# Four shared tiles with a float32 and a float32r name for what is transposed, in a two-layer hybrid decoder trunk

## Chip, core and metric

The kernel runs on one core of a Trainium2 chip. The metric is the device time of one execution in microseconds. An execution of the kernel before takes 2374.29 us (median of 3 runs, 2373.88 to 2375.04).

The core has five engines with a queue each, which the profile names PE (TensorE: matrix products and transposes; PEld is its load of the stationary operand), DVE (VectorE), ACT (ScalarE), POOL (GpSimd) and SP (SyncE, here an issuer of transfers). SBUF is the working memory, PSUM the memory that TensorE writes.

## The reference

Two layers over x of 256 positions by 2048 channels, float32, each followed by a SwiGLU FFN of hidden width 5632.

```python
for layer in range(2):
    h = rms_norm(x, mix_norm[layer])
    if layer == 0:
        z, xbc, dt_raw, c_q, c_kv, k_rope = split(h @ w_in)
        y_ssd = ssd_mixer(z, xbc, dt_raw, ...)   # conv(xbc), silu, chunked scan, rms_norm(y * silu(z))
        y_mla = mla_mixer(c_q, c_kv, k_rope, ...) # rms_norm(c_q) @ w_uq, rms_norm(c_kv) @ w_ukv, rope, softmax
        mix = concat(y_ssd, y_mla) @ w_out_even
    else:
        mix = stick_breaking_mixer(h, w_qkv, w_out_odd)   # 16 heads of 128, weights from a reversed cumsum
    x = x + mix
    h = rms_norm(x, ffn_norm[layer])
    x = x + (silu(h @ w_gate) * (h @ w_up)) @ w_down
return rms_norm(x, final_norm)
```

## The kernel before

**Precision.** A float32 product of full accuracy is made from float32r operands (the type that TensorE streams faster): each operand is split into a high part, cast to float32r by ScalarE (L330), and a low part, the rest, by VectorE (L336). Three products hi x hi, hi x lo and lo x hi are summed in PSUM. Weights arrive from HBM in tiles of 128 x 4 x 512 words (1 MB), and every tile is split so. Small products, in attention heads and the scan, are made in plain float32.

**Products.** `project` (L433) makes two 128 x 512 blocks with 16 steps of six matmuls (L440, L442, L443), one step for each 128 rows of the weights. `pair` (L733) makes two neighbouring blocks of 512 columns at once by a scheme of seven products in place of eight, M1 to M7, on part of the depth, with plain products (c0 to c3) for the rest; its matmuls have line L770. The sums of M1, M5, M6 and M7 are copied out of their bank in between ("kept", L791) and are handed later to the callbacks `left` and `right`, which add the bank's final sum to them. HALF, MORE and LATE are three orders of the same work.

**Order.** TensorE's instructions run in the order in which the program writes them. The order on the other engines is a planner's, from priorities and estimated times; `urgent` gives an instruction a high priority, and weight casts of later tiles are issued after urgent instructions. Work that has to happen while a product runs (transposes, heads, scan steps) is written as a generator; `tick` is called once or twice a step of a product and advances those that are due, and `yield n` means n ticks later. So a transpose that "waits 10" is put into TensorE's stream ten ticks into the product that follows.

**Tiles.** Most temporaries come from one pool of 42 tiles of 128 x 512 words (`s2`, named `s` in the profile). A tile is given back when all that read it are done. One arena holds the weight slots and the residual; the residual's four blocks have two names for the same memory, `xres` (float32) and `xwords` (float32r).

**Transposes.** A transpose is a TensorE instruction with the tile as the stationary operand and an identity as the moving one; its result goes to a PSUM tile `tr`. Four of 128 x 128 fill a block. `transpose` (L338) takes the float32r path (L341, `ident_r`) if the source has that type and the float32 path (L343, `ident`) if not. On the float32 path before:
- L379, `transpose_plain`: q and k of the stick-breaking layer, two tasks one after the other
- L343 on `s`: the latents c_q and c_kv and the four gated outputs of the scan
- L1338, `conv`: the inputs of the convolution, six blocks
- L1478, `evac_rope`: the rotated queries of MLA, four groups
- L343 on `xres`, L1407, L1513, L1371 and some single ones.

On the float32r path: the residual (`xwords`), and the gated tiles of the FFN (`ident_r,s`). For the latter, `right` multiplies into the tile of silu(gate) (L915), then a transfer from GpSimd's queue copies that tile into a float32r tile (L918), which is transposed ten ticks into the next product.

Of the kernel before, what the change touches and what calls it, by code (L numbers as in the profile page):

```python
# [15 lines left out]
P = 128  # L16
# [22 lines left out]


class Trunk:

# [81 lines left out]
    def weight_slots(self):  # L124
# [4 lines left out]
        base = -(-nc.sbuf_base // 256) * 256  # L129
        nc.alloc_sbuf_tensor("arena", [P, n * 2048 + 4096], F32, align_bytes=256)  # L130
        self.slots = {"wh": [], "w": [], "wsum": []}
# [11 lines left out]
        self.xres = [x(j, "xres", F32) for j in range(4)]  # L143
        self.xwords = [x(j, "xwords", F32R) for j in range(4)]

        self.saved = [self.dp.tile([P, 2, 512], F32, name=f"saved{j}") for j in range(4)]
# [225 lines left out]
    def transpose_plain(self, src, res, wait=4):  # L372

        for k2 in range(2):
            yield wait if k2 == 0 else 1
            pt = self.tr([2, S])
            for k in range(2):
                for t in range(2):
                    self.nc.tensor.transpose(pt[:, k, t * P:(t + 1) * P], src(t, 2 * k2 + k), self.ident)  # L379
# [352 lines left out]

    def pair(self, st, va, vb, left, right, order=HALF, after=lambda m: None):  # L733

# [39 lines left out]
        def add(b, x, w, keep=None):  # L774
# [13 lines left out]
            if keep:  # L788
                with self.urgent():
                    o = kept[keep] = self.s2([512])  # L790
                    copied = nc.scalar.copy(o, ps[b]).ins  # L791
# [107 lines left out]
    def ffn(self, layer, st, gain_next):  # L899
# [13 lines left out]
        def right(t, c, s):  # L913
            nc.vector.tensor_tensor(s, c, s, op=ALU.add)
            nc.vector.scalar_tensor_tensor(h[t], s, rstd[:, t:t + 1], h[t], op0=ALU.mult, op1=ALU.mult)  # L915

            words = self.s2([512], F32R)
            nc.gpsimd.dma_start(words.bitcast(F32), h[t])  # L918
            h[t] = words

        def gate_up(n):
            self.pair(st, self.cols(wg, n * 512), self.cols(wu, n * 512), left, right,
                      self.MORE if n >= 3 else self.HALF,
                      lambda m: st["lo"] if n == 0 and m in ("M3", "M6") else None)
# [75 lines left out]
    def stick(self, st):  # L1000
# [4 lines left out]
        for g in range(4):  # L1005
            raw = [[None, None], [None, None]]
            self.pair(st, cols(0, g), cols(1, g), take(raw[0]), take(raw[1]))
            qk, wts = [], []
            for r in raw:
# [70 lines left out]
    def scaled(self, st, func=AF.Copy):  # L1080

        nc = self.nc

        def to(res):
            def take(t, c, s):
                if "rstd" not in st:
                    st["rstd"] = self.norm_end(st)
                nc.vector.tensor_tensor(s, c, s, op=ALU.add)
                nc.scalar.activation(s, s, func, scale=st["rstd"][:, t:t + 1])
                res[t] = s  # L1090
            return take
# [52 lines left out]
    def even(self, st):  # L1144
# [6 lines left out]
        for n in (4, 5, 0, 1, 2, 3):  # L1151
            ps = self.project(xT, self.cols(win, OFF_XBC + n * 512, first=n == 4), KD)
            if n == 4:
                self.late_vectors()
                rstd = self.norm_end(st)
            raw = self.evac(ps, AF.Copy, rstd)
            res = []
            conv[n] = (self.spawn(self.conv(raw, n, res)), res)
            if n == 4:
# [6 lines left out]
        for off, g in ((OFF_CQ, self.g_q), (OFF_CKV, self.g_kv)):  # L1166
            ps = self.project(xT, self.cols(win, off), KD)
            raw = self.evac(ps, AF.Copy, rstd)
            ssq = self.small([P, 2], "ssqc")
# [6 lines left out]
            cT.append((self.spawn(self.transpose_split(  # L1176
                lambda t, k, raw=raw: raw[t][:, k * P:(k + 1) * P], res, g, 6)), res))
        ssq_u = self.small([P, 2, 4], "ssq")
        uT = self.operand()
        for n in range(4):  # L1180
# [3 lines left out]
            for t in range(2):  # L1184
                nc.gpsimd.tensor_tensor(y[n][t], y[n][t], sz[t], op=ALU.mult)
                if n < 3:
                    self.square_sum(y[n][t], ssq_u[:, t, n:n + 1])
            src, g = lambda t, k, n=n: y[n][t][:, k * P:(k + 1) * P], self.g_ssd[:, 4 * n:4 * n + 4]
            if n < 2:
# [7 lines left out]
        def root():  # L1197
            yield 7
            for t in range(2):
                with self.tc.issue_after(self.kept):  # L1200
                    self.square_sum(y[3][t], ssq_u[:, t, 3:4])
            yield 4
# [20 lines left out]
    def dt_and_krope(self, rstd, xT):  # L1223
# [74 lines left out]

        self.kpeT = self.small([P, 2, S], "kpeT", bufs=1)
        nc.vector.memset(self.kpeT, 0.0)  # L1300
# [12 lines left out]
    def apply_rope(self, dst, src, t, h):  # L1313
# [4 lines left out]
        a, b = src[:, :, 0:32], src[:, :, 32:64]  # L1318
        t1, t2 = (self.small([P, h, 32], f"rope{c}{h}") for c in "ab")
# [4 lines left out]
        t1, t2 = (self.small([P, h, 32], f"rope{c}{h}") for c in "ab")  # L1324
# [4 lines left out]
    def conv(self, raw, n, res):  # L1329

        nc = self.nc
        for k2 in range(2):
            yield (8 if n == 4 else 2) if k2 == 0 else 1
            pt = self.tr([2, S])
            for k in range(2):
                for t in range(2):
                    c = (2 * k2 + k) * P
                    nc.tensor.transpose(pt[:, k, t * P:(t + 1) * P], raw[t][:, c:c + P], self.ident)  # L1338
            o = self.s2([2, S])
# [92 lines left out]
    def mla_group(self, g, cq, ckv, oT):  # L1432
# [11 lines left out]

        qp = self.evac_rope(self.project(cq, heads(wuq, 128, 64), 4, 256))
        q = self.project_T(cq, heads(wuq, 0, 128))
# [16 lines left out]

    def evac_rope(self, ps):

        nc = self.nc
        rp, res = self.s2([2, 4, 64]), []
        qp = self.s2([2, 4, 64])
# [4 lines left out]
        def gen():  # L1473
            yield 7
            pt = self.tr([2, S])
            for h in range(2):
                for t in range(2):
                    nc.tensor.transpose(pt[:, h, t * P:(t + 1) * P],  # L1478
                                        rp[:, t, 2 * h:2 * h + 2].rearrange("p a d -> p (a d)"), self.ident)
            o = self.s2([2, S])  # L1480
# [93 lines left out]
```

## Time and profile before

| | |
|---|---|
| time, median of 3 | 2374.29 us |
| time of the profiled execution | 2374.24 us |
| its span, first to last instruction | 2372.2 us |
| DMA | 497.88 MB, mean 210 GB/s |
| largest group on VectorE | L336 on w, x399, 895.9 us |
| largest group on ScalarE | L330 from w, x399, 744.2 us |
| instructions of GpSimd | 301 |

Busy time of an engine is the union of its instructions; matmuls are pipelined, so the next begins before the last ends, and a busy TensorE need not be at its peak. A group of the profile is given by line, engine, operation, output and inputs by the program's names, shape, count, then busy time, mean duration in ns, and the idle time of the engine just ahead of it with what ended that idle time.

### The profile page before, as it was taken

The numbers are of one execution on the slowest core, as the hardware profiler recorded it, in microseconds if no ns is written. First come the engines' busy times: TensorE is split into PE (matmuls) and PEld (weight loads), VectorE is DVE, ScalarE is ACT, GpSimd is POOL, SyncE is SP. The second block draws the span as 40 slices with busy tenths as digits, with TensorE's granted clock in tenths as the row PEclk, the third lists the DMA queues.
The fourth block names the chain that finished last, engine by engine and source line by source line (L and its number), as shares of the span: only waits on it lengthen the run. The fifth ranks groups of instructions, "written<-read, shape, count | busy, mean of one in ns | idle before, by whom it ended". The sixth has DMA issues, their size and how long they took to land.

```text
span 2372.2 us, 28286 instructions
## 1 busy us (share of the span) xinstructions
PE 2354.9 (99%) x11083; PEld 1959.4 (83%) x11083; DVE 1987.8 (84%) x1639; ACT 1458.9 (62%) x1476; POOL 227.2 (10%) x301
## 2 busy tenths in 40 slices
PE   9999999999999999999999999999999999999998
PEld 7888888988888888888888888888888888888886
DVE  6786587588998889989888889779997988999884
ACT  6665565566665665566665686776665666556663
POOL 1341011110000000000000000000000000000011
PEclk9999999999999999999999999999999999999999
DMA  7665556445667777777776555556667777777773
GB/s 270 205 199 178 179 195 190 131 142 195 231 223 213 236 225 229 225 236 225 230 240 220 200 167 177 179 174 234 229 229 220 224 236 229 226 223 238 224 258 114
DMA packets 274917, 497.88 MB, mean 210 GB/s; under 512 B 22940, under 2 KB 48160, under 8 KB 274784
## 3 DMA queue, kind: packets, MB, share of 16 engines
q1 hardware_dynamic: 255264, 446.20, 57.2%
q0 software_dynamic: 18752, 48.55, 7.7%
q8 instruction: 87, 1.43, 0.2%
q10 hardware_dynamic: 768, 1.33, 0.2%
q14 instruction: 46, 0.38, 0.0%
HBM read 459.24 MB, written 25.20 MB: 204 GB/s over the span
## 4 chain that ended last, share of the span: by engine, by line
PE 89%; issue 6%; DVE 2%; ACT 2%; POOL 0%; DMA 0%; SPq 0%; POOLq 0%; ACTq 0%; DVEq 0%
PE acc L770 51%; PE acc L440 11%; PE acc L443 11%; PE acc L442 10%; PE acc L484 1%; DVE w L336 1%; ACT wh L330 1%; PE tr L341 1%; PE at L1423 1%; PE acc L486 0%; DVE wsum L717 0%; PE tr L343 0%; DVE wsum L336 0%; PE at L1495 0%; PE at L1496 0%
## 5 line engine op out<-in xcount | busy, mean ns | idle before, releaser
L336 DVE TENSOR_TENSOR w<-w,wh 128x2048 fp32r<-128x2048 f32 (+2 forms) x399 | 895.9, 2253 | 191.4 <-ACT wh L330 186.2
L770 PE MATMUL acc<-wh,s 128*128 128x512 f32 x3896 | 985.6, 391 | 4.2 <-ACT s L791 2.6
L330 ACT CAST wh<-w 128x2048 fp32r<-128x2048 f32 (+2 forms) x399 | 744.2, 1874 | 331.0 <-PE acc L443 154.1
L770 PEld LDWEIGHTS acc<-wh,s 128*128 128x128 f32 x3896 | 725.4, 188 | 154.2 <-ACT s L791 4.3
L440 PE MATMUL acc<-wh,s 128*128 128x512 f32 (+1 forms) x1216 | 483.6, 398 | 0.0
L443 PE MATMUL acc<-wh,s 128*128 128x512 f32 (+1 forms) x1216 | 471.5, 388 | 0.0
L442 PE MATMUL acc<-w,s 128*128 128x512 f32 (+1 forms) x1152 | 445.9, 387 | 0.0
L770 PE MATMUL acc<-w,s 128*128 128x512 f32 x1312 | 355.8, 390 | 0.5 <-DVE w L336 0.4
L770 PEld LDWEIGHTS acc<-w,s 128*128 128x128 f32 x1312 | 246.0, 188 | 53.1 <-DVE w L336 1.7
L443 PEld LDWEIGHTS acc<-wh,s 128*128 128x128 f32 x1216 | 228.7, 188 | 47.7
L440 PEld LDWEIGHTS acc<-wh,s 128*128 128x128 f32 x1216 | 228.9, 188 | 44.9 <-issue 1.7
L442 PEld LDWEIGHTS acc<-w,s 128*128 128x128 f32 x1152 | 217.1, 188 | 42.3 <-issue 1.7
L336 DVE TENSOR_TENSOR wsum<-wsum,wh 128x2048 fp32r<-128x2048 f32 (+1 forms) x101 | 218.1, 2160 | 6.3 <-ACT wh L330 6.3
L330 ACT CAST wh<-wsum 128x2048 fp32r<-128x2048 f32 (+1 forms) x101 | 182.7, 1809 | 50.2 <-PE acc L770 26.6
L330 ACT CAST wh<-lent 128x2048 fp32r<-128x2048 f32 (+1 forms) x62 | 114.5, 1857 | 61.7 <-PE acc L443 24.0
L336 DVE TENSOR_TENSOR lent<-lent,wh 128x2048 fp32r<-128x2048 f32 (+1 forms) x62 | 137.1, 2217 | 10.4 <-ACT wh L330 10.2
L717 DVE TENSOR_TENSOR wsum<-w,wsum 128x2048 f32<-128x2048 f32 (+1 forms) x52 | 104.3, 2005 | 20.2 <-PE acc L770 18.2
L791 ACT COPY s<-acc 128x512 f32<-128x512 f32 x132 | 77.3, 587 | 70.6 <-PE acc L770 70.6
L770 PE MATMUL acc<-wsum,s 128*128 128x512 f32 x380 | 104.6, 390 | 0.3 <-DVE wsum L336 0.3
L918 POOL DMA_DIRECT2D s<-s x44 | 24.4, 556 | 808.9 <-DVE s L915 465.4
L935 POOL DMA_DIRECT2D saved<-s x64 | 56.5, 1010 | 314.7 <-ACT s L934 313.6
L770 PEld LDWEIGHTS acc<-wsum,s 128*128 128x128 f32 x380 | 71.2, 188 | 16.0 <-DVE wsum L336 1.1
(270 smaller groups left out, 1924.7 us busy)
## 6 DMA issues: line engine op xcount, KB each, us to landing
w<-in_w_down_dram SPq DMA_DIRECT2D x80, 1024.0 KB, 4.9
w<-in_w_gate_dram SPq DMA_DIRECT2D x76, 1024.0 KB, 5.1
w<-in_w_up_dram SPq DMA_DIRECT2D x76, 1024.0 KB, 5.2
w<-in_w_qkv_dram SPq DMA_DIRECT2D x48, 1024.0 KB, 5.0
w<-in_w_in_dram SPq DMA_DIRECT2D x47, 1024.0 KB, 5.2
w<-in_w_out_even_dram SPq DMA_DIRECT2D x32, 1024.0 KB, 4.9
saved<-s POOLq DMA_DIRECT2D x64, 256.0 KB, 7.3
w<-in_w_out_odd_dram SPq DMA_DIRECT2D x16, 1024.0 KB, 4.9
```

The source lines that it names most:

```text
L330: cast = nc.scalar.copy(hi, src).ins
L336: return nc.vector.tensor_tensor(lo, src, hi.bitcast(F32), op=ALU.subtract).ins
L341: self.nc.tensor.transpose(out.bitcast(F32R), src, self.ident_r)
L440: nc.tensor.matmul(ps[t], hi[:, ts], wh, start=k == 0, stop=False)
L442: slot.used(nc.tensor.matmul(ps[t], hi[:, ts], wl, start=False, stop=False), self.clock)
L443: nc.tensor.matmul(ps[t], lo[:, ts], wh, start=False, stop=k == nk - 1)
L484: nc.tensor.matmul(ps[:, h % 2], wh[:, hs], x, start=k == n == 0, stop=False)
L717: ins = self.nc.vector.tensor_tensor(half(o, so), half(p, sp), half(q, sq), op=ALU.subtract).ins
L770: m = nc.tensor.matmul(ps[b], x, y, start=b not in started, stop=stop, skip_group_check=True)
L791: copied = nc.scalar.copy(o, ps[b]).ins
L918: nc.gpsimd.dma_start(words.bitcast(F32), h[t])
L935: nc.gpsimd.dma_start(self.saved[n][:, t], s, accum_op=ALU.add)
```

## The change

Four tiles (`twins`) of 128 x 512 words are laid out in the arena, each with two names for the same memory, `raw` (float32) and `words` (float32r). Engines write `raw`; TensorE transposes `words`. They are not from the pool: there is one buffer of each, so a new write waits for the readers of the last. Twins 2 and 3 share their memory with `kpeT` and with the scratch of the rotation, which are used in the first mixer only and leave the pool `small`. The pool `acts` has 40 tiles in place of 42.

- FFN: the kept sums M1 and M7 go to twins 2 and 3, where silu is applied in place; `right` multiplies into twins 0 and 1. The copy by transfer (L918) is gone.
- Stick-breaking layer: q goes to twins 0 and 1, k to twins 2 and 3.
- First mixer: convolution inputs, latents and gated outputs go to twins 0 and 1, the rotated queries to twin 0 or 1 in turn.

```diff
+class Twin:
+    def __init__(self, raw, words):
+        self.raw, self.words = raw, words
...
-        self.ap = ec(tc.tile_pool(name="acts", bufs=42))
+        self.ap = ec(tc.tile_pool(name="acts", bufs=40))
...
+        self.kpeT = more("kpeT", [P, 2, S], 2)
+        self.rope4 = {c: [more(f"rope{c}4{q}", [P, 4, 32], 3, 1024 * m + 512 * q) for q in range(2)]
+                      for m, c in enumerate("ab")}
+        self.twins = [Twin(more(f"twin{t}", [P, 512], t), more(f"twinwords{t}", [P, 512], t, 0, F32R))
+                      for t in range(4)]
...
 (transpose_plain)
-                    self.nc.tensor.transpose(pt[:, k, t * P:(t + 1) * P], src(t, 2 * k2 + k), self.ident)
+                    self.transpose(pt[:, k, t * P:(t + 1) * P], src(t, 2 * k2 + k))
...
-    def evac(self, ps, func=AF.Copy, scale=None):
+    def evac(self, ps, func=AF.Copy, scale=None, twins=None):
...
-            o = self.s2([512])
+            o = twins[t].raw if twins else self.s2([512])
...
 (pair)
-                    o = kept[keep] = self.s2([512])
+                    o = kept[keep] = homes[keep] if keep in homes else self.s2([512])
...
 (ffn)
-            nc.vector.scalar_tensor_tensor(h[t], s, rstd[:, t:t + 1], h[t], op0=ALU.mult, op1=ALU.mult)
-
-            words = self.s2([512], F32R)
-            nc.gpsimd.dma_start(words.bitcast(F32), h[t])
-            h[t] = words
+            nc.vector.scalar_tensor_tensor(self.twins[t].raw, s, rstd[:, t:t + 1], h[t], op0=ALU.mult, op1=ALU.mult)
...
+                      {"M1": self.twins[2].raw, "M7": self.twins[3].raw})
...
-                lambda t, k, h=tuple(h): h[t][:, k * P:(k + 1) * P], res, wait=10 if n < HID // 512 - 1 else 6, rank=self.URGENT)), res
+                lambda t, k: self.twins[t].words[:, k * P:(k + 1) * P], res, wait=10 if n < HID // 512 - 1 else 6, rank=self.URGENT)), res
...
 (stick, and scaled, which writes twins[t].raw where it is given twins)
-            self.pair(st, cols(0, g), cols(1, g), take(raw[0]), take(raw[1]))
+            self.pair(st, cols(0, g), cols(1, g), take(twins=self.twins[:2]), take(twins=self.twins[2:]))
...
-                    lambda t, k, r=r: r[t][:, k * P:(k + 1) * P], res)), res))
+                    lambda t, k, r=r: r[t].words[:, k * P:(k + 1) * P], res)), res))
...
 (even)
-            raw = self.evac(ps, AF.Copy, rstd)
+            raw = self.evac(ps, AF.Copy, rstd, self.twins)
...
-                nc.gpsimd.tensor_tensor(y[n][t], y[n][t], sz[t], op=ALU.mult)
+                nc.gpsimd.tensor_tensor(self.twins[t].raw, y[n][t], sz[t], op=ALU.mult)
...
 (conv)
-                    nc.tensor.transpose(pt[:, k, t * P:(t + 1) * P], raw[t][:, c:c + P], self.ident)
+                    self.transpose(pt[:, k, t * P:(t + 1) * P], self.twins[t].words[:, c:c + P])
...
 (evac_rope)
-                    nc.tensor.transpose(pt[:, h, t * P:(t + 1) * P],
-                                        rp[:, t, 2 * h:2 * h + 2].rearrange("p a d -> p (a d)"), self.ident)
+                    self.transpose(pt[:, h, t * P:(t + 1) * P], twin.words[:, (2 * t + h) * P:(2 * t + h + 1) * P])
```

More of the change, by code (lines that the diff above doesn't have):

```diff
@@ L144, in weight_slots @@
         self.xwords = [x(j, "xwords", F32R) for j in range(4)]
+        more = lambda name, shape, t, o=0, dt=F32: nc.alloc_sbuf_tensor_at(
+            name, shape, dt, offset=base + 8192 * n + 16384 + 2048 * t + o).ap()
+        self.kpeT = more("kpeT", [P, 2, S], 2)
[3 more added lines that the diff above has]
+                      for t in range(4)]
         self.saved = [self.dp.tile([P, 2, 512], F32, name=f"saved{j}") for j in range(4)]
@@ L731, with pair @@
     LATE = ("M1", "M5", "M3", "M6", "M2", "M7", "M4", "c0", "c1", "c2", "c3")
-    def pair(self, st, va, vb, left, right, order=HALF, after=lambda m: None):
+    def pair(self, st, va, vb, left, right, order=HALF, after=lambda m: None, homes={}):
         nc = self.nc
@@ L1082, in scaled, with to @@
         nc = self.nc
-        def to(res):
+        def to(res=None, twins=None):
             def take(t, c, s):
@@ L1088, in take @@
                 nc.vector.tensor_tensor(s, c, s, op=ALU.add)
-                nc.scalar.activation(s, s, func, scale=st["rstd"][:, t:t + 1])
-                res[t] = s
+                o = twins[t].raw if twins else s
+                nc.scalar.activation(o, s, func, scale=st["rstd"][:, t:t + 1])
+                if res:
+                    res[t] = s
             return take
@@ L1167, in even @@
             ps = self.project(xT, self.cols(win, off), KD)
-            raw = self.evac(ps, AF.Copy, rstd)
+            raw = self.evac(ps, AF.Copy, rstd, self.twins)
             ssq = self.small([P, 2], "ssqc")
@@ L1176, in even @@
             cT.append((self.spawn(self.transpose_split(
-                lambda t, k, raw=raw: raw[t][:, k * P:(k + 1) * P], res, g, 6)), res))
+                lambda t, k: self.twins[t].words[:, k * P:(k + 1) * P], res, g, 6)), res))
         ssq_u = self.small([P, 2, 4], "ssq")
@@ L1200, in root @@
                 with self.tc.issue_after(self.kept):
[L1201 removed]
+                    self.square_sum(self.twins[t].raw, ssq_u[:, t, 3:4])
             yield 4
@@ L1318, in apply_rope, with pair @@
         a, b = src[:, :, 0:32], src[:, :, 32:64]
-        t1, t2 = (self.small([P, h, 32], f"rope{c}{h}") for c in "ab")
+        def pair():
+            if h != 4:
+                return tuple(self.small([P, h, 32], f"rope{c}{h}") for c in "ab")
+            for c in "ab":
+                self.rope4[c].append(self.rope4[c].pop(0))
+            return tuple(self.rope4[c][1] for c in "ab")
+        t1, t2 = pair()
         tt = nc.gpsimd.tensor_tensor
@@ L1323, in apply_rope @@
         tt(dst[:, :, 0:32], t1, t2, op=ALU.subtract)
-        t1, t2 = (self.small([P, h, 32], f"rope{c}{h}") for c in "ab")
+        t1, t2 = pair()
         tt(t1, a, sin, op=ALU.mult)
```

22 lines of the change are left out of this document (10 added, 12 removed).

## Prediction, made before the result was known

> **What bounds the kernel now.** I read the page first, then TensorE's waits, then the busy time by stage.
>
> ```profile
> span 2372.2 us, 28286 instructions
> PE 2354.9 (99%) x11083; PEld 1959.4 (83%) x11083; DVE 1987.8 (84%) x1639; ACT 1458.9 (62%) x1476; POOL 227.2 (10%) x301
> PEclk9999999999999999999999999999999999999999
> ```
> ```profile
> engine line waited for: us in total, times, longest us
> PE acc L770 <- ACT s L791: 2.6, 3, 1.2
> PE tr L293 <- DVE s L253: 1.8, 1, 1.8
> PE acc L770 <- ACT wh L330: 1.6, 1, 1.6
> PE tr L341 <- PE tr L341: 0.9, 1, 0.9
> PE tr L343 <- DMA xres<-in_x_dram: 0.6, 1, 0.6
> PE acc L770 <- DVE w L336: 0.4, 2, 0.2
> PE acc L770 <- DVE wsum L336: 0.3, 1, 0.3
> ```
> ```profile
> 34.00:205.00 171.00, 171.00 (x866) 142.12 (x867) 129.83 (x232) 107.36 (x121) 54.11 (x59) 1.00 0.60 199
> 410.00:520.00 110.00, 109.57 (x759) 100.93 (x757) 66.59 (x110) 63.78 (x132) 23.48 (x43) 1.00 0.49 148
> 640.00:1190.00 550.00, 550.00 (x2474) 455.22 (x2473) 493.91 (x305) 327.92 (x255) 37.65 (x50) 1.00 0.73 226
> 1340.00:1580.00 240.00, 237.99 (x1126) 198.93 (x1125) 199.55 (x160) 174.22 (x213) 18.00 (x16) 1.00 0.53 173
> ```
>
> The columns of the last block are: stretch and its length, then busy time with count of TensorE, weight load, VectorE, ScalarE and GpSimd. TensorE is busy 99% of the span at the full granted clock. All that it waited for another instruction or a transfer adds up to 2.6 + 1.8 + 1.6 + 0.9 + 0.6 + 0.4 + 0.3 = 8.2 us, and 2.4 of these (the idle tile of L253 and the first load of x) belong to the start. In the convolution stretch it is busy 171.00 of 171.00 us, in the first FFN 550.00 of 550.00. So the rule for this change is simple: an edit counts if it makes TensorE's own queue shorter, or if it puts a wait into that queue. What the other engines gain is not seen in the end time.
>
> **What gets shorter: 176 transposes.** The diff gives four tiles a second, float32r name, so five groups of transposes leave the float32 path (ident) for the float32r path (ident_r). The rows of these groups, and the one of the FFN's activations that take the float32r path already:
>
> ```profile
> L341 PE MATMUL tr<-ident_r,s 128*128 128x128 f32 x176 | 20.1, 237 | 0.0
> L379 PE MATMUL tr<-ident,s 128*128 128x128 f32 x64 | 8.3, 272 | 0.0
> L343 PE MATMUL tr<-ident,s 128*128 128x128 f32 x48 | 7.4, 273 | 0.0
> L1338 PE MATMUL tr<-ident,s 128*128 128x128 f32 x48 | 7.2, 272 | 0.0
> L1478 PE MATMUL tr<-ident,s 128*128 128x128 f32 x16 | 2.4, 272 | 0.0
> ```
>
> These are q and k (L379), the latent and gated outputs (L343), the convolution inputs (L1338) and the rotated queries (L1478): 64 + 48 + 48 + 16 = 176. Other float32 transposes (L1407, L1513 and a few more) are left as they are. The mean duration of one, 272 against 237 ns, is not the price: transposes overlap, and what counts is by how much a group pushes back the matmuls behind it. This is read from the timeline, in two places where a group of four, then four 128x512 matmuls of L770, then the next group of four follow each other. First float32, then float32r (columns: start, duration of the merged row, instructions):
>
> ```profile
> 612.76 0.60 PE L343 MATMUL tr<-ident,xres 128*128 128x128 f32 x4
> 613.11 1.17 PE L770 MATMUL acc<-wh,s 128*128 128x512 f32 x4
> 614.12 0.60 PE L343 MATMUL tr<-ident,xres 128*128 128x128 f32 x4
> ```
> ```profile
> 707.51 0.85 PE L770 MATMUL acc<-w,s 128*128 128x512 f32 x3
> 708.20 0.46 PE L341 MATMUL tr<-ident_r,s 128*128 128x128 f32 x4
> 708.49 1.16 PE L770 MATMUL acc<-wh,s 128*128 128x512 f32 x4
> 709.49 0.46 PE L341 MATMUL tr<-ident_r,s 128*128 128x128 f32 x4
> ```
> ```profile
> 1347.52 1.03 PE L379 MATMUL tr<-ident,s 128*128 128x128 f32 x8
> 1348.31 1.17 PE L770 MATMUL acc<-wh,s 128*128 128x512 f32 x4
> 1349.32 0.93 PE L379 MATMUL tr<-ident,s 128*128 128x128 f32 x7
> ```
>
> From group to group the float32 case takes 614.12 - 612.76 = 1.36 us, the float32r case 709.49 - 708.20 = 1.29 us, with the same four matmuls inside. Four transposes become 0.07 us cheaper (0.06 to 0.08 within the rounding of the starts). A matmul of L770 takes (708.20 - 707.51) / 3 = 0.23 us, so four transposes cost 1.36 - 0.92 = 0.44 us in float32 and 0.37 in float32r.
>
> In the stick-breaking layer the transposes of q and k stand together, eight at a time (the third block; its last row is cut at seven by the end of the window): 1349.32 - 1347.52 - 0.92 = 0.88 us for eight. In float32r eight should cost at most twice four, 0.74, and at least 8 x (708.49 - 708.20) / 4 = 0.58, plus the 0.37 - 0.29 = 0.08 us by which the matmul behind a group is late, 0.66. They save 0.14 to 0.22; I take 0.17, nearer to the price of the fours, which is measured.
>
> The sum: 112 transposes outside the stick-breaking layer are 28 groups of four, 28 x 0.07 = 2.0 us; 64 in it are 8 groups of eight, 8 x 0.17 = 1.4 us. Together 3.4 us, all on TensorE's queue, which does not wait where they stand (171.00 of 171.00; 109.57 of 110.00; 237.99 of 240.00). From the bounds: 28 x 0.06 + 8 x 0.14 = 2.8, and 28 x 0.08 + 8 x 0.22 = 4.0.
>
> One float32 transpose lasts 272 ns, yet four behind each other cost 0.44 us, not four times 272: what each spends on latency is overlapped. [...]
>
> **What goes away on GpSimd.** In the FFN each gated tile was copied by a transfer into a float32r tile (L918) before it was transposed.
>
> ```profile
> L918 POOL DMA_DIRECT2D s<-s x44 | 24.4, 556 | 808.9 <-DVE s L915 465.4 <-issue 301.4 <-ACT s L791 41.2
> L336 DVE TENSOR_TENSOR s<-tr,s 128x512 fp32r<-128x512 f32 x44 | 29.8, 687 | 19.5 <-DMA saved<-s 14.7 <-issue 2.9 <-ACT s L330 1.7
> ```
>
> 44 issues of 0.556 us and 44 transfers disappear, on a queue that is 10% busy. TensorE's list of waits has no row for these copies, and L341 has 0.0 idle ahead of it: the transposes are put ten steps of the next product later, and that covers the transfer. Value 0. The accumulating transfers of L935 that share the queue wait for ScalarE, not for these. The second row shows VectorE waiting 14.7 us for acts tiles that a transfer still reads; with two words tiles and two kept tiles fewer per block, 40 buffers in place of 42 are not scarcer. It is worth 0 too, since TensorE is 550.00 of 550.00 there.
>
> **What waits are added.** A twin is one buffer, so each new write waits for the readers of the last. For most that is long past: q and k are read in the first steps of the next pair (1347.52 and 1349.32 above) and written again at its end; the convolution inputs are read three steps into a product of sixteen. The close one is in the FFN. The first kept product (M1, L791) now goes to twin 2, which becomes the silu result that the product of gate and up (L915) reads. Where two gate-up pairs follow each other without a down projection (blocks 0 to 1 and 1 to 2, two layers: four places), ScalarE's copy of M1 must wait for the last L915:
>
> ```profile
> 696.81 1.41 DVE L915 SCALAR_TENSOR_TENSOR s<-s,rstd,s 128x512 f32<-128x512 f32 x2
> 697.51 0.59 ACT L791 COPY s<-acc 128x512 f32<-128x512 f32 x1 [1.67 <-PE acc L770]
> 698.00 1.92 ACT L330 CAST wh<-wsum 128x2048 fp32r<-128x2048 f32 x1
> 704.74 2.29 DVE L336 TENSOR_TENSOR wsum<-wsum,wh 128x2048 fp32r<-128x2048 f32 x1
> ```
>
> L915 ends at 698.22, so the copy starts 0.7 us later than at 697.51, and the cast behind it as much. That cast is of M6's weights, whose low part VectorE takes at 704.74, after the cast's end at 699.92: 4.8 us of slack. The bank that the copy frees is written next by M6, after the 48 matmuls of M5, c0 and M3, 48 x 0.23 = 11 us on. Cost 0; without that cover it would be 4 x 0.7 = 2.8 us.
>
> The order on ScalarE, VectorE and GpSimd comes from a planner that works with estimated times, so it may shift in places that the diff does not touch. The nearest price is what TensorE waits after its start, 8.2 - 2.4 = 5.8 us: I let it move by up to 3 us either way and take 0.
>
> **Forecast.** The profiled execution took 2374.24 us (its span and 2.0 around it), next to the median of 2374.29; 2374.24 - 3.4 = 2370.8 us, 0.14% less. About 0.2%, 4.7 us, is what a measurement of this kernel can tell from no change, so this counts as within.
>
> **The rivals.**
> - No gain: the float32r transposes are as slow at these places, because the load of the stationary tile (140 ns for L341, nearly the same in float32) sets the pace. For: the durations differ by only 35 ns. Against: the two periods of 1.36 and 1.29. It gives 2374.2. With the forecast it fills the middle case.
> ```profile
> L341 PEld LDWEIGHTS tr<-ident_r,s 128*128 128x128 f32 x176 | 19.8, 140 | 5.8
> L379 PEld LDWEIGHTS tr<-ident,s 128*128 128x128 f32 x64 | 7.5, 141 | 1.1
> ```
> - Faster: the new order on ScalarE also removes the 2.6 us in which TensorE waits for kept copies (L791). For: more free acts tiles, and kept copies without a pool tile. Against: the three places lie in output projections, whose pairs get no twins. It gives 2374.2 - 3.4 - 2.6 = 2368.2.
> - Slower: M1's copy holds up ScalarE's in-order queue, and the casts behind it come too late. It decides when L915 ends over 4.8 us after M1's last product, which takes three 2.29 us low parts ahead of it on VectorE, busy 493.91 of 550.00. Then 3 x 2.29 - 4.8 = 2.1 us are lost at each of the four places, 8.4 in all: 2374.2 - 3.4 + 8.4 = 2379.2, 5.0 slower than before. Against: L915 is marked urgent, and in the rows it ends 0.7 us after M1's last product.
>
> **Chances.** Forecast 0.60, no gain 0.08, faster 0.23, slower 0.09. Only more than 4.7 us counts as faster, so the faster case needs 1.3 us beyond the 3.4, about half of those 2.6. The range goes from 2374.2 - 4.0 - 2.6 = 2367.6 up to 2374.2 - 2.8 + 3 = 2374.4, with the no-gain case in it; the slower case and the far end of the faster one are left out.
>
> **What would show it.** Right: L379, L1338, L343 on s and L1478 gone from the float32 groups, 440 transposes with ident_r in L341 (264 now, xwords with them), 0.37 us for four and 0.66 to 0.74 for eight in the timeline, no row of L918, TensorE still at 550 of 550 in the FFN, its waits near 8 us. Wrong: a new row in TensorE's waits for ScalarE or VectorE of over 3 us; eight q and k transposes that still take 0.88; or the span shorter by more than the groups explain.

## The result and the profile after

The change makes the kernel slower. After: 2388.72 us, median of 6 (2388.11 to 2390.78); before, beside it: 2374.33 us, median of 6 (2373.88 to 2375.43). The ratio is 1.0061 [1.0048, 1.0074], 14.4 us more, where 3.4 us less was forecast. The profiled execution of after took 2388.3 us, its span is 2386.6.

The page of after: span, busy time and count of each engine.

```profile
span 2386.6 us, 28174 instructions
PE 2357.8 (99%) x11083; PEld 1958.5 (82%) x11083; DVE 1985.7 (83%) x1639; ACT 1460.5 (61%) x1478; POOL 208.1 (9%) x257
```

TensorE runs the same 11083 instructions. Its idle time went from 2372.2 - 2354.9 = 17.3 to 2386.6 - 2357.8 = 28.8 us, 11.5 more, and its busy time grew by 2.9 although the transposes became shorter: two things to explain, not one. Next, what TensorE waited for in after:

```profile
PE tr L356 <- DVE twin L1187: 5.3, 2, 3.1
PE acc L785 <- ACT s L806: 4.7, 5, 1.2
PE tr L356 <- POOL twin L1198: 2.4, 1, 2.4
...
PE acc L785 <- DVE wsum L351: 1.5, 2, 0.7
PE at L1292 <- DVE adt L1288: 1.3, 1, 1.3
...
PE tr L1426 <- ACT s L1368: 0.5, 1, 0.5
```

(Lines shifted by 15 to 19: L356 is the float32r path of `transpose`, L341 before; L345 the cast, L351 the low part, L408 the evacuation, L341 the square sum, L785 and L806 the matmuls and kept copies of `pair`.) With the rows not shown the list adds up to 19.1 us against 8.2 before. Two rows are new and large, both for tiles that the change renamed: the transposes of the two latents wait 5.3 us for their scaling (L1187), and those of one gated output wait 2.4 us for GpSimd's product (L1198). Both lie in one stretch of the first mixer. First before, then after (columns as in the prediction's block of stretches):

```profile
205.00:320.00 115.00, 115.00 (x540) 94.94 (x539) 70.82 (x67) 58.50 (x68) 12.82 (x9) 1.00 0.55 179
```
```profile
205.00:320.00 115.00, 107.02 (x488) 87.25 (x487) 62.07 (x61) 52.31 (x59) 10.31 (x8) 0.96 0.49 161
640.00:1190.00 550.00, 549.27 (x2465) 454.44 (x2463) 496.10 (x310) 335.98 (x259) 24.46 (x28) 1.00 0.71 219
```

In 205 to 320 TensorE gets through 488 instructions in place of 540, waits 8 us, and its granted clock is 0.96 instead of 1.00. The FFN is as full as before but for one wait of 0.73 us in its first block. As the 11083 instructions stand in the same order in both traces, I subtracted start from start, one by one: after is 1.3 us behind at 75 us and still at 205, 8.4 at 260, 13.6 at 320, 14.4 at 600 and 14.4 at the end. So 7.1 us are lost around the latents, 5.2 around the third gated output, 1.3 at the wait for `adt` at 75 us, and 0.8 net in the rest; each figure is already net of the transposes saved there.

The saving is there. Two groups of eight in the stick-breaking layer of after, with four matmuls between them:

```profile
1362.65 0.79 PE L356 MATMUL tr<-ident_r,twinwords 128*128 128x128 f32 x8
1363.28 1.18 PE L785 MATMUL acc<-wh,s 128*128 128x512 f32 x4
1364.29 0.79 PE L356 MATMUL tr<-ident_r,twinwords 128*128 128x128 f32 x8
```

1364.29 - 1362.65 - 0.92 = 0.72 us for eight; the prediction had 0.88 before and 0.66 to 0.74 after. Averaged over all groups, each measured by how much later the matmuls behind it start, four transposes become 0.077 us cheaper and eight 0.179: 28 x 0.077 + 8 x 0.179 = 3.6 us.

### The profile page after: what moved, and what is told of

Its sections match the earlier page's. It is cut to its first block, busy times and chain, and to the rows that moved or that the text cites. A ratio compares the mean times of both kernels' runs of the same rounds, so it can differ in the third digit from the quotient of the medians.

```text
span 2386.6 us, 28174 instructions
## 1 busy us (share of the span) xinstructions
PE 2357.8 (99%) x11083; PEld 1958.5 (82%) x11083; DVE 1985.7 (83%) x1639; ACT 1460.5 (61%) x1478; POOL 208.1 (9%) x257
## 4 chain that ended last, share of the span: by engine, by line
PE 86%; issue 7%; DVE 3%; ACT 3%; DMA 1%; POOL 0%; POOLq 0%; ACTq 0%; DVEq 0%
PE acc L785 49%; PE acc L455 10%; PE acc L457 10%; PE acc L458 10%; ACT wh L345 1%; PE tr L356 1%; DVE w L351 1%; PE acc L499 1%; DVE wsum L732 1%; PE at L1442 1%; PE acc L501 0%; PE at L1513 0%; PE at L1514 0%; POOL spare L1122 0%; PE at L1073 0%
## 5 line engine op out<-in xcount | busy, mean ns | idle before, releaser
L351 DVE TENSOR_TENSOR w<-w,wh 128x2048 fp32r<-128x2048 f32 (+2 forms) x399 | 892.1, 2244 | 203.2 <-ACT wh L345 197.2
L785 PE MATMUL acc<-wh,s 128*128 128x512 f32 x3896 | 985.7, 391 | 4.9 <-ACT s L806 4.7
L345 ACT CAST wh<-w 128x2048 fp32r<-128x2048 f32 (+2 forms) x399 | 743.8, 1874 | 339.9 <-PE acc L458 152.2
L785 PEld LDWEIGHTS acc<-wh,s 128*128 128x128 f32 x3896 | 725.5, 188 | 155.2 <-ACT s L806 6.8
L785 PE MATMUL acc<-w,s 128*128 128x512 f32 x1312 | 356.0, 390 | 0.3 <-DVE w L351 0.2
L785 PEld LDWEIGHTS acc<-w,s 128*128 128x128 f32 x1312 | 246.0, 188 | 52.9 <-DVE w L351 1.6
L351 DVE TENSOR_TENSOR wsum<-wsum,wh 128x2048 fp32r<-128x2048 f32 (+1 forms) x101 | 218.0, 2158 | 9.0 <-ACT wh L345 9.0
L345 ACT CAST wh<-wsum 128x2048 fp32r<-128x2048 f32 (+1 forms) x101 | 182.8, 1810 | 51.4 <-PE acc L785 23.8
L345 ACT CAST wh<-lent 128x2048 fp32r<-128x2048 f32 (+1 forms) x62 | 114.5, 1856 | 61.6 <-PE acc L458 30.5
L351 DVE TENSOR_TENSOR lent<-lent,wh 128x2048 fp32r<-128x2048 f32 (+1 forms) x62 | 137.1, 2216 | 11.0 <-ACT wh L345 10.5
L785 PE MATMUL acc<-wsum,s 128*128 128x512 f32 x380 | 104.6, 390 | 1.5 <-DVE wsum L351 1.5
L785 PEld LDWEIGHTS acc<-wsum,s 128*128 128x128 f32 x380 | 71.2, 188 | 17.2 <-DVE wsum L351 2.3
L806 ACT COPY s<-acc 128x512 f32<-128x512 f32 x88 | 51.5, 587 | 40.2 <-PE acc L785 40.2
L732 DVE TENSOR_TENSOR wsum<-w,w 128x2048 f32<-128x2048 f32 (+1 forms) x35 | 71.4, 2039 | 2.0 <-DMA w<-in_w_qkv_dram 1.4
```

The costliest lines, as they stand in the source:

```text
L345: cast = nc.scalar.copy(hi, src).ins
L351: return nc.vector.tensor_tensor(lo, src, hi.bitcast(F32), op=ALU.subtract).ins
L732: ins = self.nc.vector.tensor_tensor(half(o, so), half(p, sp), half(q, sq), op=ALU.subtract).ins
L785: m = nc.tensor.matmul(ps[b], x, y, start=b not in started, stop=stop, skip_group_check=True)
```

## The experiments

Three theories stood against each other. A: the order on ScalarE around the latents has changed, because their evacuation needs no tile of the pool any more. B: a twin is a single buffer, and a write waits for the readers of its last contents. C: with 40 tiles in place of 42 the pool runs short where `silu(z)` is evacuated. Twelve kernels were run; all build on after or on its repair `urg_sz`.

| kernel | what it is | median us (range, n) | ratio to before [95%] |
|---|---|---|---|
| urg | after, latents' norm urgent | 2379.09 (2377.52 to 2379.80, 10) | 1.0019 [1.0009, 1.0029] |
| gate | after, gated outputs in pool tiles again | 2387.79 (2385.93 to 2390.82, 4) | 1.0059 [1.0044, 1.0074] |
| sz | after, silu(z) in idle spare tiles | 2383.28 (2380.33 to 2384.27, 5) | 1.0035 [1.0022, 1.0048] |
| urg_sz | both | 2374.04 (2373.61 to 2374.96, 10) | 0.9999 [0.9990, 1.0009] |
| f32 | urg_sz, float32 path for the twins but the FFN's | 2377.17 (2376.47 to 2377.74, 10) | 1.0011 [1.0002, 1.0021] |
| ffn | urg_sz, the FFN's copies by transfer back | 2376.07 (2375.60 to 2377.07, 10) | 1.0006 [0.9997, 1.0015] |
| lat | after, latents in pool tiles again | 2379.84 (2378.38 to 2380.72, 10) | 1.0022 [1.0012, 1.0031] |
| wait | after, latents' transposes 5 ticks later | 2380.14 (2378.49 to 2381.84, 10) | 1.0022 [1.0012, 1.0031] |
| swap | after, square sums behind both evacuations | 2379.46 (2377.76 to 2380.83, 10) | 1.0021 [1.0011, 1.0030] |
| best1 | urg_sz, dt chain urgent | 2374.00 (2372.85 to 2374.80, 10) | 0.9997 [0.9988, 1.0006] |
| best2 | best1, convolution urgent too | 2380.34 (2378.95 to 2381.63, 10) | 1.0024 [1.0014, 1.0033] |
| best3 | urg_sz, two groups of matmuls two ticks later | 2373.63 (2373.38 to 2374.57, 11) | 0.9996 [0.9988, 1.0005] |

Before's medians beside them: 2374.24 (first four), 2374.55 (f32, ffn, best1, best2), 2374.46 (lat, wait), 2374.50 (swap, best3).

**The latents: an order on ScalarE.** The rows of ScalarE around the latent c_q before, with the scaling on VectorE and the transposes that it must beat:

```profile
199.15 1.31 ACT L393 ACTIVATE s<-acc,rstd 128x512 f32<-128x512 f32 x2 [3.87 <-PE acc L443]
200.36 1.90 ACT L330 CAST wh<-w 128x2048 fp32r<-128x2048 f32 x1
...
203.50 1.28 ACT L314 ACT_TABLE_LOAD   x1
...
206.10 0.88 DVE L1174 TENSOR_SCALAR s<-s,rstd 128x512 f32<-128x512 f32 x2
...
208.62 0.60 PE L343 MATMUL tr<-ident,s 128*128 128x128 f32 x4
```

Both evacuations, a cast, both square sums, the square root's table, and the scaling ends at 206.98, 1.64 us before TensorE comes to the transposes. The same place in after:

```profile
200.39 0.69 ACT L408 ACTIVATE twin<-acc,rstd 128x512 f32<-128x512 f32 x1 [3.79 <-PE acc L458]
201.11 0.63 ACT L341 ACTIVATE s<-twin 128x512 f32<-128x512 f32 x1
...
201.74 0.67 ACT L408 ACTIVATE twin<-acc,rstd 128x512 f32<-128x512 f32 x1
202.31 1.90 ACT L345 CAST wh<-w 128x2048 fp32r<-128x2048 f32 x1
...
204.11 0.63 ACT L341 ACTIVATE s<-twin 128x512 f32<-128x512 f32 x1
...
206.51 1.91 ACT L345 CAST wh<-w 128x2048 fp32r<-128x2048 f32 x1 [1.68 <-PE acc L458]
208.44 1.28 ACT L329 ACT_TABLE_LOAD   x1
208.45 2.29 DVE L351 TENSOR_TENSOR w<-w,wh 128x2048 fp32r<-128x2048 f32 x1 [1.84 <-ACT wh L345]
...
211.65 0.88 DVE L1187 TENSOR_SCALAR twin<-twin,rstd 128x512 f32<-128x512 f32 x2
...
212.28 0.99 PE L356 MATMUL tr<-ident_r,twinwords 128*128 128x128 f32 x4 [2.19 <-DVE twin L1187]
```

One square sum (201.11) now stands between the evacuations. Through it the second square sum ends at 204.7, and the planner has put a weight cast ahead of the table load. That cast needs a slot that TensorE is still reading; ScalarE stands idle for 1.68 us, and the table load behind the cast comes at 208.44, when the cast is done (206.51 + 1.91 = 208.42), instead of 203.50. The reciprocal that follows on VectorE then stands behind a low part of 2.29 us. The scaling ends at 212.53, 5.55 us later than before; 1.64 of cover and the lateness of TensorE itself are not enough, and it waits 2.19 us. At the second latent it is 3.09.

Four runs test this. *urg* keeps everything and gives the norm priority:

```diff
+            with self.urgent():
                 for t in range(2): self.square_sum(raw[t], ssq[:, t:t + 1])
                 r = self.rstd(ssq, 512)
                 for t in range(2): nc.vector.tensor_scalar(raw[t], raw[t], r[:, t:t + 1], None, op0=ALU.mult)
```

> The changed kernel (2388.7 us), with the whole chain between the latents' evacuation and their transposes (square sums, reciprocal root, scaling) marked urgent. Three theories. A, order: the chain is late because the planner put a square sum between the two evacuations and a weight cast ahead of the square root on ScalarE; then the two stalls of TensorE ahead of the latents' transposes go, with the slow matmuls behind them, 8.4 - 1.3 = 7.1 us by the offsets between the two traces: 2381.6. B, one buffer: the writes into the twins wait for the readers of the last contents; priority doesn't change that: 2388.7. C, pool: 40 tiles in place of 42 are too few and hold up whatever needs a tile: 2388.7, since the chain needs the same tiles.

Measured: 2379.09, 9.6 us less than after. The table load and the scaling in urg:

```profile
203.43 1.28 ACT L329 ACT_TABLE_LOAD   x1
...
205.95 0.89 DVE L1188 TENSOR_SCALAR twin<-twin,rstd 128x512 f32<-128x512 f32 x2
```

The row of L1187 is gone from TensorE's waits, that of GpSimd's product stays, with 2.4 at the longest. The latents are a matter of order, with the single buffers untouched. It is 2.5 us better than A expected (2381.6). By the starts of the two traces, 7.6 us come back at the latents and 2.6 at the third stall, where the wait is the same but no half clock follows it (granted clock 1.00 from 305 to 323 in urg; last section).

*lat* puts the latents back into pool tiles, with float32 transposes, in a pool that still has 40:

```diff
-            raw = self.evac(ps, AF.Copy, rstd, self.twins)
+            raw = self.evac(ps, AF.Copy, rstd)
```

> The changed kernel (2388.7 us) with only the two latents taken back: they go to pool tiles and are transposed in float32 as before; the pool keeps its 40 tiles. If the twin is what lets the first evacuation run early, so that the planner puts a square sum between the two, the old order comes back and both stalls ahead of the latents' transposes go, with the slow matmuls: 2388.7 - 7.1 - (0 to 2.5 if the clock stays up at the third stall) + 4 x 0.07 = 2379.4 to 2381.9, near the 2379.1 of the urgent chain. If the pool of 40 makes the latents late, taking two more tiles from it makes it worse: over 2388.7.

Measured: 2379.84. The order of before comes back, both evacuations first, and neither latent is waited for. So 40 tiles are enough here, and C falls for the latents. Why the planner orders an evacuation into a twin otherwise than one into a pool tile is not shown.

*wait* leaves the order as after has it and moves the transposes from 6 to 11 ticks into the next product:

```diff
-                lambda t, k: self.twins[t].words[:, k * P:(k + 1) * P], res, g, 6)), res))
+                lambda t, k: self.twins[t].words[:, k * P:(k + 1) * P], res, g, 11)), res))
```

> The changed kernel with the latents' transposes put 11 ticks into the next product in place of 6, the order of the other engines left to the planner. The chain ends some 5.5 us later than before the change against a cover of 1.6 us; five ticks are 5 x 6 x 0.23 = 6.9 us. So if the stalls are only a chain that is longer than its cover, both go: 2379 to 2382. If the chain waits for the transposes or for a buffer, it moves along with them: 2388.7.

Measured: 2380.14, the waits for the latents are gone: the chain is longer than its cover, and it does not move along with its readers.

*swap* only holds the square sums until the second evacuation is issued:

```diff
+            copied = self.pressing[-1][1]
...
+                with self.tc.issue_after(copied):
-                self.square_sum(raw[t], ssq[:, t:t + 1])
+                    self.square_sum(raw[t], ssq[:, t:t + 1])
```

> The changed kernel (2388.7 us) with one order fixed: the square sums of the latents are issued after the second evacuation, not between the two. Twins, pool and float32r transposes stay. If that one square sum ahead of its turn sets off the rest (the first weight cast is then ahead of the other square sum, and the next cast ahead of the square root), both stalls ahead of the latents' transposes go: 2379 to 2382, like the urgent chain (2379.1). If the casts would go ahead of the square root in any case, 2388.7, less 0.7 at most.

Measured: 2379.46. ScalarE in swap:

```profile
200.89 1.37 ACT L408 ACTIVATE twin<-acc,rstd 128x512 f32<-128x512 f32 x2 [3.79 <-PE acc L458]
202.16 1.90 ACT L345 CAST wh<-w 128x2048 fp32r<-128x2048 f32 x1
...
205.31 1.28 ACT L329 ACT_TABLE_LOAD   x1
```

That is before's order, with twins and 40 tiles: one activation of 0.63 us put back in its turn undoes all the rest. It is not the loss by itself. In urg it still stands between the evacuations, at 201.30, but no weight cast stands ahead of the table load.

**The third gated output: tiles of the pool.** The rows of after ahead of its wait:

```profile
306.94 0.62 ACT L345 CAST s<-s 128x512 fp32r<-128x512 f32 x1 [6.25 <-PE acc L458]
...
309.66 0.69 ACT L408 ACTIVATE s<-acc,rstd 128x512 f32<-128x512 f32 x1 [0.72 <-PE acc L458]
...
312.98 0.69 ACT L408 ACTIVATE s<-acc,rstd 128x512 f32<-128x512 f32 x1 [2.63 <-DVE s L351]
...
315.12 0.62 PE L356 MATMUL tr<-ident_r,twinwords 128*128 128x128 f32 x3 [2.39 <-POOL twin L1198]
```

Before, both evacuations of silu(z) stand together:

```profile
298.69 1.27 ACT L393 ACTIVATE s<-acc,rstd 128x512 f32<-128x512 f32 x2 [5.73 <-PE acc L443]
```

TensorE is 8.4 us behind here, so 298.69 would be 307.1. In after the first evacuation comes at 309.66, the second at 312.98. At the head of ScalarE's queue stands a cast whose output tile TensorE still reads (6.25), and the second evacuation gets a tile that a low part is still reading (2.63, <-DVE s L351). Both are tiles of the pool, which speaks for C; B would blame the single twin that GpSimd writes behind them.

*gate* takes the twin away from this place:

```diff
-                nc.gpsimd.tensor_tensor(self.twins[t].raw, y[n][t], sz[t], op=ALU.mult)
+                nc.gpsimd.tensor_tensor(y[n][t], y[n][t], sz[t], op=ALU.mult)
```

> The changed kernel with the gated outputs taken back: each is multiplied in place into its own pool tile and transposed in float32; everything else stays. A, order: the third stall (ahead of the third gated block, 5.3 us with the slow matmuls behind it) has to do with the order of the latents and not of this part: about as before, 2388.7 + 8 x 0.07 = 2389.3. B, one buffer: the third stall is the product's wait for its twin: 5.3 go, 0.6 come back, 2384.0. C, pool of 40 tiles: the stall stays, since now even more tiles are held: 2389.3 or more.

Measured: 2387.79, and the stall is still there. Its row of TensorE's waits in gate:

```profile
PE tr L358 <- POOL s L1198: 2.5, 2, 2.3
```

B falls. *sz* keeps the twins and takes two tiles of demand off the pool; for that the scan task has to be joined ahead of the evacuation, a change of order as well:

```diff
-            sz = self.evac(ps, AF.Silu, rstd)
             self.join(ssd[n])
+            sz = self.evac(ps, AF.Silu, rstd, [Twin(s, None) for s in self.spare[2 * n:2 * n + 2]])
```

> The changed kernel with silu(z) of the four gated blocks written to idle spare tiles outside the pool, so that the pool has two tiles more at that stage; the twins stay. C, pool: the third stall goes, 2388.7 - 5.3 = 2383.4. A and B: no change, 2388.7.

Measured: 2383.28, 5.4 us less than after; no row for L1198 any more. The two evacuations in sz:

```profile
305.12 1.37 ACT L408 ACTIVATE spare<-acc,rstd 128x512 f32<-128x512 f32 x2 [2.85 <-PE acc L458]
```

They wait for TensorE's product alone. Together with the rows of after this says that the pool is short at this place. The run alone does not prove it, since its edit changes an order too, and whether 42 tiles beside the twins would have sufficed was not tried. One more wait goes with the edit: five waits for kept copies, 4.7 us, become four, 3.6; the fifth was 1.16 us at 348.9 in after.

**Both together, and what the transposes are worth.** *urg_sz* has both edits. It tells whether the two losses are all of it:

> Both together: the latents' chain urgent, and silu(z) in spare tiles. A and C together: 2388.7 - 7.1 - 5.3 = 2376.3. B: 2388.7.

Measured: 2374.04, 2.3 us less than A and C together expected. The offsets of 7.1 and 5.3 were net of the transposes saved there, 0.5 us at each place, and the kept copy, 1.0 by the offsets, was not in them. The two single gains give 9.6 + 5.4 = 15.0 of 14.7 us; that they add up so well is in part luck, since a stall that stays in one run costs a different stretch of half clock in another (at the third stall 6.83 us in after, none in urg). But the kernel is now equal to before, not 3.6 faster. The difference lies in small rows of TensorE's waits, here those of urg_sz:

```profile
PE acc L785 <- ACT s L806: 3.6, 4, 1.2
...
PE acc L785 <- DVE wsum L351: 1.4, 2, 0.7
PE at L1293 <- DVE adt L1289: 1.3, 1, 1.3
...
PE tr L1427 <- ACT s L1369: 0.5, 1, 0.5
```

Before had 2.6 for the first, 0.3 for the second, no row for the last two, and 1.6 for a cast that is gone. In sum the list has 11.1 against 8.2 us, so 2.9 of the 3.6 are lost again in waits. Whether the faster transposes cause these waits, the next run tells.

*f32* checks that the transposes really bring something, by sending those of the convolution, latents, gated outputs, rotated queries, q and k through the float32 path from the same tiles (`.raw` for `.words`):

```diff
-                    lambda t, k, r=r: r[t].words[:, k * P:(k + 1) * P], res)), res))
+                    lambda t, k, r=r: r[t].raw[:, k * P:(k + 1) * P], res)), res))
...
```

> The mended kernel urg_sz (2374.0 us) with the 176 transposes of the twins back on the float32 path: the tile's float32 name is transposed instead of its float32r name, everything else stays, the FFN too. If the price read from the timeline is right (0.44 against 0.37 us for four, 0.88 against about 0.71 for eight), this takes 3.4 us more: 2377.4. If latency sets the price whatever the type, 2374.0.

Measured: 2377.17; with before's median 0.3 higher beside it, 2.8 us more than urg_sz. A group of eight in f32:

```profile
1349.68 1.04 PE L358 MATMUL tr<-ident,twin 128*128 128x128 f32 x8
1350.47 1.17 PE L785 MATMUL acc<-wh,s 128*128 128x512 f32 x4
1351.48 1.03 PE L358 MATMUL tr<-ident,twin 128*128 128x128 f32 x8
```

1351.48 - 1349.68 - 0.92 = 0.88 us again. Two rows of f32's waits are shorter than in urg_sz:

```profile
PE acc L785 <- ACT s L806: 2.6, 3, 1.1
PE at L1293 <- DVE adt L1289: 0.7, 1, 0.7
```

The cast of 1.6 us is back, and the whole list has 10.4 us, 0.7 less than in urg_sz: slower transposes give the other engines time. 3.6 - 0.7 = 2.9, close to the 2.8 measured. "No gain" falls.

The run shows one thing more. With the old price of the transposes f32 is still 2.6 us slower than before [1.0002, 1.0021], and its waits are 10.4 against 8.2. So of the 2.9 us lost again in urg_sz only 0.7 go with the faster transposes; 2.2 come with the tiles and with the order that they bring; after has the same rows already. Start by start f32 falls behind before at four places: by 1.0 us at 75 (adt), 0.7 at 136, 0.7 at 628 and 0.4 at 1692, the last two in the first blocks of the FFNs.

*ffn* puts the 44 copies by transfer back:

```diff
-            nc.vector.scalar_tensor_tensor(self.twins[t].raw, s, rstd[:, t:t + 1], h[t], op0=ALU.mult, op1=ALU.mult)
+            nc.vector.scalar_tensor_tensor(h[t], s, rstd[:, t:t + 1], h[t], op0=ALU.mult, op1=ALU.mult)
+            words = self.s2([512], F32R)
+            nc.gpsimd.dma_start(words.bitcast(F32), h[t])
+            h[t] = words
```

> The mended kernel urg_sz (2374.0 us) with the FFN's 44 copies by transfer put back (the product is made in place in twins 2 and 3 and copied into a float32r pool tile, which is transposed). If the copies lie beside other work, as the prediction has it: 2374.0, within 1. If the pool theory also holds for the FFN, the two tiles more in each block hold up ScalarE there: a new wait of TensorE in the FFN, over 2 us.

Measured: 2376.07, with the same correction 1.7 us more than urg_sz, between what the two theories expected. That is at the edge of what medians can tell, but there is a row for it:

```profile
PE acc L785 <- DVE lent L351: 1.0, 2, 0.7
```

Start by start, this kernel falls back by 0.7 us at 676 and by 1.1 at 1740, early in the two FFNs. With 40 tiles, doing without the copies is worth somewhat under 2 us, not 0.

**Three attempts to keep the gain.** *best1* makes the chain of dt urgent, *best2* the convolution steps too:

```diff
-            conv[n] = (self.spawn(self.conv(n, res)), res)
+            conv[n] = (self.spawn(self.conv(n, res), self.URGENT), res)
...
-                self.dt_task = self.spawn(self.dt_and_krope(rstd, xT))
+                self.dt_task = self.spawn(self.dt_and_krope(rstd, xT), self.URGENT)
```

> urg_sz with the chain of dt (up to the adt tile that TensorE waits for at about 75 us) at urgent priority too. Order theory: the 1.3 us wait for adt goes, 2374.0 - 1.4 = 2372.6. If that wait is set by the length of the chain and not by its place in VectorE's order: 2374.0.

> best1 with the convolution's steps urgent as well. Order theory: the 0.6 us stall at the first transposes of the scan goes too, 2372.0. Rival: with so much ahead of them the weight casts come late, and TensorE waits for them: over 2374.

Measured: 2374.00 for the first, the wait for adt halved to 0.7. What sets the rest is open: two low parts of 2.3 us and the convolution's multiplications still stand between the links of the urgent chain. The second is 6.3 us slower: neither theory's mechanism, but the urgent convolution pushes back the very chain that was to be helped. VectorE in best2, six multiplications of the convolution in a row between two links of the chain, twice, and the chain's end:

```profile
68.26 2.42 DVE L1367 SCALAR_TENSOR_TENSOR s<-tr,vb,s 128x255 f32<-128x255 f32 x6
70.61 0.21 DVE L1279 TENSOR_TENSOR s<-s,s 128x64 f32<-128x64 f32 x1
...
73.52 2.42 DVE L1367 SCALAR_TENSOR_TENSOR s<-tr,vb,s 128x255 f32<-128x255 f32 x6
...
80.48 0.22 DVE L1289 SCALAR_TENSOR_TENSOR adt<-dt,ea 128x64 f32<-128x64 f32 x1
```

In urg_sz that last step starts at 75.28. TensorE waits 6.1 us for it here.

*best3* leaves the priorities alone and moves the late readers two ticks back:

```diff
-        yield 11
+        yield 13
...
-        yield 3 if g else 6
+        yield 3 if g else 8
```

> urg_sz (2374.0 us, with TensorE's waits of 1.3 us for adt and 0.5 us at the scan's first transposes) with these two steps put two ticks later into TensorE's stream. If they are only late against their cover, both waits go: 2374.0 - 1.8 = 2372.2, less than the kernel before (2374.3). If they move along, 2374.0.

Measured: 2373.63 beside 2374.50, the lowest of all, though its interval holds 1. The wait for adt is gone; 0.9 and 0.6 us for other readers have come. No version here is shown to beat before.

## Why the prediction was wrong, point by point

- **The price of the transposes** held: 3.6 us measured, 3.4 forecast (2.8 to 4.0), with 0.72 us for eight. All 440 transposes with ident_r are in L356 (352 of twins, 88 of xwords), no row of L918 is left.
- **The step that failed first:** "The order on ScalarE, VectorE and GpSimd comes from a planner ..., so it may shift ... I let it move by up to 3 us either way and take 0." The bound came from what TensorE waited before, 5.8 us. That measures stalls that exist, not the slack of chains that do not stall yet. The latents' scaling had 1.64 us of cover, readable in the trace of before, and one weight cast ahead of the table load costs 1.68 + 1.91 us. The prediction's own sign of being wrong, a new wait of over 3 us for VectorE, came with L1187's 5.3. Undoing the shift or covering it is worth 8.6 to 9.6 us (wait, lat, swap, urg), more than the 7.1 lost at the latents. The rest is the clock at the third stall, as far as the profiled executions tell: none at half in lat and urg, 3.41 us in swap, but 6.83 in wait as in after. Small waits elsewhere that come with the new arrangement are worth another 2.2 us (f32); why each of them comes was not followed up.
- **The second:** "with two words tiles and two kept tiles fewer per block, 40 buffers in place of 42 are not scarcer." True of the FFN, for which it was worked out. In the first mixer's gated blocks the pool runs short, 5.4 us with the kept copy (sz); that 42 would have been enough is not shown. The part on waits looked at the FFN, q and k, and the convolution, but neither at the latents nor at silu(z).
- **A twin is one buffer:** no stall was traced to that. In the FFN the copy of M1 does wait for L930. The copy of the prediction's example, in after's timeline:

```profile
713.46 0.59 ACT L806 COPY twin<-acc 128x512 f32<-128x512 f32 x1 [2.52 <-DVE twin L930]
```

The 2.52 us are idle time of ScalarE, most of which it has before as well (1.67). TensorE is 15.14 us behind here, so the copy would start at 697.51 + 15.14 = 712.65 and is 0.81 us late, close to the 0.7 forecast. The trace shows it at two places instead of four. From 640 to 1190 us TensorE's distance to before stays at 15.14: the cover held, and "cost 0" with it.

- **Value 0 for the copies of L918** held for this change: behind the first blocks of the two FFNs TensorE neither gains nor loses on before. Only with 40 tiles would the copies cost something, under 2 us (ffn).
- **The first blocks of the FFNs** lose a little, 0.75 and 0.4 us, to low parts of `wsum` (L351) that come late. The prediction had nothing there; f32 shows that it is not the speed of the transposes.
- **The rivals:** the slower case had the right sign with the wrong mechanism and place. It put the price on M1's copy in the FFN, where the cover held. "Faster" was wrong too: TensorE's wait for kept copies rose from 2.6 to 4.7.
- **A term was missing:** TensorE's clock. Of the 2.9 us by which its busy time grew, the transposes make -3.6, and 10.24 us at half clock make +4.8 (last section); 1.7 I can't place.

## What to carry to other kernels

Where a planner orders an engine's queue, an edit that gives an instruction another output tile can change the order around it, so for every chain that ends in work of the bounding engine read its cover (when the chain ends, when its reader starts), and price a shift against that cover, not against today's stalls. When a saving does not show in the time, run the new arrangement without the saving: here 2.9 of 3.6 us were lost again, of which 0.7 because TensorE was faster, and 2.2 by the arrangement itself (f32). When a pool shrinks, look for the stage where it is emptiest, not for the stage that the edit is about.

## What the runs showed of the hardware

In after, TensorE's clock fell at two of the three stalls. Granted clock (the first figure behind GpSimd's count) around them:

```profile
211.00:217.00 6.00, 4.67 (x23) 4.02 (x24) 2.26 (x8) 0.84 (x2) 0.00 (x0) 0.72 0.00 0
240.00:246.00 6.00, 2.77 (x14) 2.00 (x13) 3.96 (x9) 1.24 (x4) 0.00 (x0) 1.00 0.43 161
313.00:319.00 6.00, 3.88 (x14) 3.20 (x15) 3.51 (x2) 4.88 (x5) 1.27 (x1) 0.62 0.15 56
319.00:325.00 6.00, 6.00 (x23) 4.83 (x23) 2.51 (x2) 3.25 (x5) 0.00 (x0) 0.81 0.41 137
```

The clock is 0.5 from 212.04 for 3.41 us and from 314.44 for 6.83 us; matmuls of 512 columns then start every 0.43 instead of 0.23 us, so 10.24 us at half clock cost 10.24 x (0.427 - 0.227) / 0.427 = 4.8 us. The first stretch begins 0.24 us before the end of the stall of 2.19 us (at 212.28), the second 0.68 us before the end of the one of 2.39 us (at 315.12). The longest stall, of 3.09 us up to 244.16, has none: the clock is 1.00 from 240 to 252. In sz and gate, where the same two stalls stand ahead of the latents' transposes (5.3 us together, 3.1 the longer), it is the other way round: the clock is 1.00 from 211 to 217, and from 240 to 246 and 246 to 252 it is 0.71 and 0.73 in sz, 0.73 and 0.70 in gate. If all of that is half clock, it makes 6 x (0.29 + 0.27) / 0.5 = 6.7 and 6 x (0.27 + 0.30) / 0.5 = 6.8 us. And the third stall, 2.4 us in urg too, has 1.00 there from 305 to 323. So neither the length of a stall nor its place in the program settles it in these runs; what does is not shown. By the price above, a stall cost 0, 1.6 or 3.2 us more in after (none, 3.41 or 6.83 us at half); I take such differences for the wider scatter of gate (4.9 us) and sz (3.9) beside urg_sz (1.4), though no run tested the scatter by itself.
